# A weight ring of its own for the feed-forward part, with blocks that begin at an offset that changes from weight tile to weight tile

## The chip, the core and the metric

The kernel runs on one core of a Trainium2 chip. Five engines work side by side on that core and wait for each other through semaphores: TensorE (PE, matmuls; PEld is its weight load), VectorE (DVE), ScalarE (ACT), GpSimd (POOL) and SyncE (SP), which here issues every DMA. The metric is the device time of one execution in microseconds, the median of several runs. The kernel before takes 856.42 us.

## The reference

One decoder layer for 512 tokens of width 1024, all in float32. A token mixer (a pooling branch and a sparse attention branch, merged by gates) comes first; behind it stands the part that the change touches:

```python
def conv_ffn(h, w_up, conv_w, conv_b, w_down):
    S = h.shape[1]
    u = h @ w_up                                   # 1024 -> 2 x 2752
    up = jnp.pad(u, ((0, 0), (CONV_WIDTH - 1, 0), (0, 0)))
    c = conv_b + conv_w[0] * up[:, 0:S]
    for tap in range(1, CONV_WIDTH):
        c = c + conv_w[tap] * up[:, tap:tap + S]
    gate, val = jnp.split(c, 2, axis=-1)
    return (jax.nn.silu(gate) * val) @ w_down      # 2752 -> 1024
...
        x = x + token_mixer(h, ...)
        h = rms_norm(x, ffn_norm_w[l])
        x = x + conv_ffn(h, w_up[l], conv_w[l], conv_b[l], w_down[l])
```

## The kernel before

Activations lie transposed: a tile holds 128 channels by 512 tokens. Every large product is made of three matmuls on rounded halves: a value is split into `hi` (its rounding) and `lo` (the rest), and `mm3` (L103 to L109) adds hi·hi, hi·lo and lo·hi in one PSUM bank. The first operand of `pe.matmul` after the bank is the stationary one (128 by 128, loaded as weights); the second moves through it, up to 512 columns at a time.

**The weight ring.** `Ring` (L146) fetches one tile of weights (128 by 1024) by DMA into `st` (two buffers), and splits it in blocks of 512 columns: ACT writes `hi` (L95), DVE writes `lo` (L98). There are six `hi` and six `lo` buffers, so three tiles of weights are in flight. One ring serves the whole kernel; it lives in the pool `wr`, opened at the start.

**The stages at the end.** After the attention come, one after another on PE: `w_ab` (eight tiles, moving operand `oT`), `w_o` (eight tiles, moving operands `mh` and `ml`), the up projection `w_up` (43 tiles, moving operands `h2h` and `h2l`, called by `conv_tile`, L795), and the down projection `w_dn` (eight output tiles `c`, each of three fetches of seven 128-column blocks, moving operands `gh` and `gl`). The last output tile of `w_dn` is computed in two halves of 256 tokens. Output tile 7 of `w_o` is added to the residual (DVE L782), then split into `h2h7`, `h2l7`; the squares of all eight are summed on POOL (L212) for the norm, whose factors are applied only after the up projection (`rstdb`). So the up projection can begin before the norm is done, and with k = 0 to 6 before the last tile of `w_o` is done.

**Order.** The program is written in Python as above; the framework then orders each engine's instructions by a simulation of its own and puts in the waits. A buffer of a tag is free for its next writer when its last reader is done. A pool that is opened where a closed pool lay may write there only when the closed pool's readers are done.

**Addresses.** In the built program the buffers begin, in each partition, at these bytes: `hi` and `lo` blocks of the ring at 79,904 + 2,048 n; `oT` tiles at 32 bytes past a multiple of 512; `mh`, `ml` at 480 past a multiple of 512; `h2h`, `h2l` at multiples of 2,048; `gh`, `gl` at 32 past a multiple of 512. Earlier in the kernel `tok_gemm` (L304, matmuls `tg`) moves ring blocks of 256 columns past stationary activations `hh` and `hl`, which lie where `h2h` and `h2l` do later, and `cmp_hid` (matmuls `hp`, L461) moves ring blocks of 256 columns past the stationary `X`, whose slices begin at 480 past a multiple of 512. A 128-column weight block is 512 bytes of a partition, so the four blocks of one buffer begin at the same byte modulo 512 (79,904 is 32 past a multiple of 512).

Of the kernel before, what the change touches and what calls it, by code (L numbers as in the profile page):

```python
# [12 lines left out]
F32R = mybir.dt.float32r  # L13
# [6 lines left out]
P = 128  # L20
# [54 lines left out]
def layer(ctx: ExitStack, tc: tile.TileContext, par, masks, xT, w_kva, w_tm, w_fm, w_pl, w_pbr,  # L75
# [5 lines left out]
    def nm(s):  # L81
        cnt[0] += 1
        return f"{s}{cnt[0]}"

    def pool(stack, name, **kw):
        return stack.enter_context(tc.tile_pool(name=name, bufs=1, **kw))
# [4 lines left out]
    def split(hi, lo, src, scale=None, eng=None, cast=None):  # L91

        if scale is None:
            if cast is None:
                a.activation(hi, src, AF.Copy)  # L95
            else:
                cast.tensor_copy(hi, src)
            (eng or v).tensor_tensor(lo, src, r32(hi), ALU.subtract)  # L98
        else:
            a.activation(hi, src, AF.Copy, scale=scale)  # L100
            v.scalar_tensor_tensor(lo, src, scale, r32(hi), ALU.mult, ALU.subtract)

    def mm3(ps, pairs, first=True, last=True):  # L103

        n = len(pairs)
        for i, ((sh, sl), (mh_, ml_)) in enumerate(pairs):
            pe.matmul(ps, sh, mh_, start=first and i == 0, stop=False)  # L107
            pe.matmul(ps, sh, ml_, start=False, stop=False)  # L108
            pe.matmul(ps, sl, mh_, start=False, stop=last and i == n - 1)  # L109
# [2 lines left out]
    cp = pool(ctx, "cp")  # L112
    xp = pool(ctx, "xp")
    ypp = pool(ctx, "ypp")
    wr = pool(ctx, "wr")
    mix = ExitStack()
    qo = pool(mix, "qo")
    kvp = pool(mix, "kvp")
# [10 lines left out]
    def bank(p, tag, name, bufs):  # L129
        return p.tile([P, S], F32, tag=tag, name=nm(name), bufs=bufs)  # L130
# [13 lines left out]


    class Ring:  # L146
        def __init__(self, p, half, bufs):
            self.p, self.half, self.bufs = p, half, bufs

        def __call__(self, src, w, n, eng=None, cast=None):  # L150

            st = self.p.tile([P, 1024], F32, tag="st", name=nm("st"), bufs=self.bufs[0])
            nc.sync.dma_start(st[:, :n * w], src)
            out = []
            per = self.half // w
            for i in range(0, n, per):
                m = min(per, n - i)
                hi = self.p.tile([P, self.half], F32R, tag="hi", name=nm("hi"), bufs=self.bufs[1])
                lo = self.p.tile([P, self.half], F32R, tag="lo", name=nm("lo"), bufs=self.bufs[1])
                split(hi[:, :m * w], lo[:, :m * w], st[:, i * w:(i + m) * w], eng=eng, cast=cast)  # L160
                out += [(hi[:, j * w:(j + 1) * w], lo[:, j * w:(j + 1) * w]) for j in range(m)]
            return out

    ring = Ring(wr, 512, (2, 6))
# [590 lines left out]
    mh = [pq.tile([P, S], F32R, name=f"mh{c}") for c in range(8)]  # L755
    ml = [pq.tile([P, S], F32R, name=f"ml{c}") for c in range(8)]

    def fm2(src, ht, hl_):
        ps = bank(psm, "m", "fm", 6)
        mm3(ps, [(w, (ht[k], hl_[k])) for k, w in enumerate(ring(src, P, KC))])  # L760
        return ps

    for c in range(8):
        if c < NF1:
            z = sg1[c]
        else:
            z = sig2(fm2(w_fm[12 + c], hh, hl), pq.tile([P, S], F32, tag="zg", name=nm("zg"), bufs=2))
        ya = fm2(w_ab[c], oh, ol)
        v.scalar_tensor_tensor(z, z, 1.0, ya, ALU.add, ALU.mult)
        v.scalar_tensor_tensor(z, z, 0.5, ypool[c], ALU.mult, ALU.add)  # L770
        split(mh[c], ml[c], z)

    x1 = [ypp.tile([P, S], F32, tag=f"yp{c}", name=f"x1_{c}") for c in range(8)]
    h2h = [xp.tile([P, S], F32R, tag=f"hh{k}", name=f"h2h{k}") for k in range(KC)]
    h2l = [xp.tile([P, S], F32R, tag=f"hl{k}", name=f"h2l{k}") for k in range(KC)]
# [4 lines left out]
    for c in range(8):  # L780
        ps = fm2(w_o[c], mh, ml)
        v.tensor_tensor(x1[c], ps, x1[c], ALU.add)  # L782
        split(h2h[c], h2l[c], x1[c], fn[:, c:c + 1])
        sq_add(ssum, x1[c], c, pq, g, 4)
# [2 lines left out]
    mix.close()  # L787


    fp = pool(ctx, "fp")  # L790
    gh = [fp.tile([P, S], F32R, name=f"gh{j}") for j in range(NG - 1)]
    gl = [fp.tile([P, S], F32R, name=f"gl{j}") for j in range(NG - 1)]
    gs = fp.tile([P, S], F32R, name="gs")

    def conv_tile(t):  # L795
        ps = fm2(w_up[t], h2h, h2l)
        u = fp.tile([P, S], F32, tag="u", name=nm("u"), bufs=2)
        v.tensor_tensor(u, ps, rstdb, ALU.mult)
        c = fp.tile([P, S], F32, tag="c", name=nm("c"), bufs=3)
        a.activation(c, u, AF.Identity, bias=conv[:, t, 3:4], scale=conv[:, t, 2:3])  # L800
        v.scalar_tensor_tensor(c[:, 1:], u[:, :S - 1], conv[:, t, 1:2], c[:, 1:], ALU.mult, ALU.add)
        v.scalar_tensor_tensor(c[:, 2:], u[:, :S - 2], conv[:, t, 0:1], c[:, 2:], ALU.mult, ALU.add)
        return c

    for j in range(NG):
        if j == 0:
            c = conv_tile(0)
            rows = 64
            cv = fp.tile([P, S], F32, tag="c", name=nm("cv"), bufs=3)
            a.activation(cv[:64], c[64:128], AF.Copy)  # L810
            cg = c
        else:
            cg = conv_tile(2 * j - 1)
            cv = conv_tile(2 * j)
            rows = P
        a.activation(cg[:rows], cg[:rows], AF.Silu)
        v.tensor_tensor(cg[:rows], cg[:rows], cv[:rows], ALU.mult)
        if j == 0:
            split(gs[:64], gs[64:], cg[:64])
        else:  # L820
            split(gh[j - 1], gl[j - 1], cg)
# [7 lines left out]
    for c in range(8):  # L829
        sl = slice(c * P, (c + 1) * P)  # L830

        cols = [slice(0, S)] if c < 7 else [slice(h * S // 2, (h + 1) * S // 2) for h in range(2)]
        banks = [bank(psm, "m", "dn", 6) for _ in cols]
        ws = []
        for q_ in range(3):
            ws += ring(w_dn[c, :, q_ * 896:(q_ + 1) * 896], P, 7)
            if q_ < 2:
                for ps, cs in zip(banks, cols):
                    mm3(ps[:, cs], [(ws[k], (gh[k][:, cs], gl[k][:, cs])) for k in range(7 * q_, 7 * q_ + 7)],
                        first=q_ == 0, last=False)  # L840
        for ps, cs in zip(banks, cols):
            mm3(ps[:, cs], [(ws[k], (gh[k][:, cs], gl[k][:, cs])) for k in range(14, 21)], first=False, last=False)
            pe.matmul(ps[:, cs], wlh[:, sl], gs[:, cs], start=False, stop=False)
            pe.matmul(ps[:, cs], wll[:64, sl], gs[:64, cs], start=False, stop=True)
            o = fp.tile([P, S], F32, tag="o", name=nm("o"), bufs=2)
            v.tensor_tensor(o[:, cs], ps[:, cs], x1[c][:, cs], ALU.add)
            nc.sync.dma_start(outT[sl, cs], o[:, cs])
# [92 lines left out]
```

## Time and profile before

| | |
|---|---|
| median of 3 runs | 856.42 us (856.03 to 857.04) |
| profiled execution, its own time | 855.8 us |
| its span, first to last instruction | 853.9 us |
| PE busy | 837.8 us (98% of the span) |
| DVE, ACT, POOL busy | 566.4, 466.5, 235.5 us |
| mean granted TensorE clock | 0.996 of full speed |

The span is what the trace covers; the 1.9 us between span and time lie around it. A matmul's duration in the profile contains its way through the array, which overlaps with the next matmul's, so what a stream of matmuls costs is read from the distance of their starts. A granted clock of 1.0 is TensorE's upper level (2.4 GHz), 0.5 the lower one (1.2 GHz).

### The profile page before, as it was taken

Reading aid. Unit: us, or ns where it says so; the run is one execution under the profiler, and the core shown is the slowest. Engines: PE = TensorE matmul, PEld = TensorE weight load, DVE = VectorE, ACT = ScalarE, POOL = GpSimd, SP = SyncE. Lnnn points to the kernel's source line nnn. Section 1 sums busy time; section 2 is a strip of 40 time slices with the busy share of each in tenths; the row PEclk is TensorE's granted clock in tenths of the full one; section 3 lists DMA queues with packets and bytes.
Section 4 is the critical chain, followed back from the end, with each engine's and each line's share of the span. In section 5 each row is a group of like instructions: output and inputs, shape, how many; then the busy total and the mean of one; then the engine's idle time right before and its main releaser. Section 6 shows DMA issues by size and latency. Waiting matters only on the chain.

```text
span 853.9 us, 12252 instructions
## 1 busy us (share of the span) xinstructions
PE 837.8 (98%) x4355; PEld 700.9 (82%) x4355; DVE 566.4 (66%) x1203; ACT 466.5 (55%) x1002; POOL 235.5 (28%) x325
## 2 busy tenths in 40 slices
PE   7999899999999999999999999999999999999998
PEld 6889888978888888888888888888888888887887
DVE  7788967777787878785555539777777777423221
ACT  6846857768787877874334437545444444322220
POOL 5796714357565655640001200000000000000000
PEclk9999989999999999999999999999999999999999
DMA  6332132321001100101443223332233323333430
GB/s 218 102 119 91 51 102 96 103 96 50 26 26 47 30 25 26 47 28 50 148 148 99 98 74 100 99 98 83 91 100 98 99 85 104 111 108 99 111 98 25
DMA packets 22972, 72.82 MB, mean 85 GB/s; under 512 B 2816, under 2 KB 3328, under 8 KB 22912
## 3 DMA queue, kind: packets, MB, share of 16 engines
q1 hardware_dynamic: 22912, 72.05, 27.5%
q8 instruction: 34, 0.56, 0.3%
q14 instruction: 26, 0.21, 0.1%
HBM read 69.94 MB, written 2.10 MB: 84 GB/s over the span
## 4 chain that ended last, share of the span: by engine, by line
PE 84%; ACT 2%; DVE 1%; issue 1%; ACTq 0%; DVEq 0%
PE fm L107 16%; PE fm L108 16%; PE fm L109 16%; PE dn L107 5%; PE op L704 5%; PE dn L108 4%; PE dn L109 4%; PE tp L697 4%; PE ss L665 2%; PE ss L666 2%; PE op L709 1%; PE sc L608 1%; PE tg L312 1%; PE hp L461 1%; PE tg L310 1%; PE tg L311 1%
## 5 line engine op out<-in xcount | busy, mean ns | idle before, releaser
L95 ACT ACTIVATE hi<-st 128x512 fp32r<-128x512 f32 (+3 forms) x253 | 152.1, 607 | 202.2 <-PE fm L108 103.6
L98 DVE TENSOR_TENSOR lo<-st,hi 128x512 fp32r<-128x512 f32 (+1 forms) x210 | 141.8, 680 | 108.5 <-ACT hi L95 104.6
L107 PE MATMUL fm<-h2h,hi 128*128 128x512 f32 x344 | 136.1, 396 | 0.0
L108 PE MATMUL fm<-h2l,hi 128*128 128x512 f32 x344 | 136.0, 396 | 0.0
L109 PE MATMUL fm<-h2h,lo 128*128 128x512 f32 x344 | 135.9, 395 | 0.0
L677 POOL TENSOR_TENSOR pb<-pb,sm 128x128 f32<-128x128 f32 (+3 forms) x128 | 90.4, 738 | 49.3 <-DVE sm L674 40.4
L655 ACT ACTIVATE pb<-pb,nm 128x384 f32<-128x384 f32 (+3 forms) x128 | 71.1, 556 | 20.0 <-DVE nm L654 19.3
L107 PEld LDWEIGHTS fm<-h2h,hi 128*128 128x128 f32 x344 | 64.6, 188 | 15.7
L108 PEld LDWEIGHTS fm<-h2l,hi 128*128 128x128 f32 x344 | 64.6, 188 | 15.5
L109 PEld LDWEIGHTS fm<-h2h,lo 128*128 128x128 f32 x344 | 64.6, 188 | 15.5
L107 PE MATMUL fm<-hh,hi 128*128 128x512 f32 x160 | 71.6, 448 | 0.0
L107 PE MATMUL dn<-gh,hi 128*128 128x512 f32 (+1 forms) x189 | 69.9, 370 | 0.0
L108 PE MATMUL dn<-gl,hi 128*128 128x512 f32 (+1 forms) x189 | 69.1, 365 | 0.0
L109 PE MATMUL dn<-gh,lo 128*128 128x512 f32 (+1 forms) x189 | 69.1, 365 | 0.0
L98 DVE TENSOR_TENSOR ptl<-tp,pth 128x512 fp32r<-128x512 f32 (+1 forms) x96 | 57.2, 597 | 14.4 <-ACT pth L95 13.9
L654 DVE CUSTOM_DVE_ANT_0 pb<-ss,mk 128x384 f32<-128x384 f32 (+3 forms) x128 | 59.5, 482 | 8.5 <-PE ss L666 4.3
L108 PE MATMUL fm<-hl,hi 128*128 128x512 f32 x160 | 63.6, 397 | 0.0
L109 PE MATMUL fm<-hh,lo 128*128 128x512 f32 x160 | 63.0, 396 | 0.0
L95 ACT ACTIVATE pth<-tp 128x512 fp32r<-128x512 f32 (+1 forms) x96 | 49.8, 518 | 20.1 <-PE tp L697 19.7
L98 POOL TENSOR_TENSOR lo<-st,hi 128x512 fp32r<-128x512 f32 x36 | 48.5, 1350 | 34.4 <-ACT hi L95 34.4
L310 PE MATMUL tg<-hi,hh 128*128 128x256 f32 x192 | 54.1, 284 | 1.1 <-ACT h L288 1.1
L311 PE MATMUL tg<-hi,hl 128*128 128x256 f32 x192 | 53.6, 282 | 0.0
(256 smaller groups left out, 1838.4 us busy)
## 6 DMA issues: line engine op xcount, KB each, us to landing
st<-in_w_up SPq DMA_DIRECT2D x43, 512.0 KB, 3.5
st<-in_w_dn SPq DMA_DIRECT2D x24, 448.0 KB, 3.4
st<-in_w_fm SPq DMA_DIRECT2D x20, 512.0 KB, 3.5
st<-in_w_tm SPq DMA_DIRECT2D x12, 512.0 KB, 3.5
st<-in_w_ab SPq DMA_DIRECT2D x8, 512.0 KB, 3.4
st<-in_w_o SPq DMA_DIRECT2D x8, 512.0 KB, 3.5
x<-in_xT SPq DMA_DIRECT2D x15, 256.0 KB, 3.7
st<-in_cw SPq DMA_DIRECT2D x4, 512.0 KB, 3.7
```

The costliest lines, as they stand in the source:

```text
L95: a.activation(hi, src, AF.Copy)
L98: (eng or v).tensor_tensor(lo, src, r32(hi), ALU.subtract)
L107: pe.matmul(ps, sh, mh_, start=first and i == 0, stop=False)
L108: pe.matmul(ps, sh, ml_, start=False, stop=False)
L109: pe.matmul(ps, sl, mh_, start=False, stop=last and i == n - 1)
L310: pe.matmul(ps[:, :n], hh[k][:, tt], H, start=k == 0, stop=False)
L311: pe.matmul(ps[:, :n], hl[k][:, tt], H, start=False, stop=False)
L654: v.tensor_tensor_reduce(p_, ps, mcaus[:, S - n:], -1.0, 3e38, ALU.add, ALU.min, nm_[:, i:i + 1])
L655: a.activation(p_, p_, AF.Exp, bias=nm_[:, i:i + 1], scale=-1.0, accum_out=sm[:, i:i + 1])
L677: g.tensor_tensor(pb[:, PBASE[i]:PBASE[i] + n], pb[:, PBASE[i]:PBASE[i] + n], sm[:, i:i + 1].to_broadcast([P, n]), ALU.mult)
L697: last = pe.transpose(tp[:, n:n + P], pb[:, PBASE[i] + j * P:PBASE[i] + (j + 1) * P], ident)
L704: pe.matmul(op[:, j * P:], V2[b][j][:, G], pt_[:, TBASE[j]:TBASE[j] + w], start=b == 0 and j == 0 and part == 0, stop=False)
```

## The change

The old ring's pool is put on a stack of its own and closed after the mixer's pools; a new pool `wr2` is opened in its place and a new ring made in it, with the same numbers of buffers. A block of the new ring is 640 columns wide instead of 512, and `Ring.at` says at which of them the 512 used columns begin: `8 * (t // 3)` for tile `t` of `w_up` (0 to 112 columns, 0 to 448 bytes, a new value each time the ring has gone round), and `8 * c + 4` for output tile `c` of `w_dn` (4 to 60 columns, 16 to 240 bytes). What is computed is the same.

```diff
-    wr = pool(ctx, "wr")
+    wrs = ExitStack()
+    wr = pool(wrs, "wr")
...
     class Ring:
-        def __init__(self, p, half, bufs):
-            self.p, self.half, self.bufs = p, half, bufs
+        def __init__(self, p, half, bufs, pad=0):
+            self.p, self.half, self.bufs, self.pad, self.at = p, half, bufs, pad, 0
...
-                hi = self.p.tile([P, self.half], F32R, tag="hi", name=nm("hi"), bufs=self.bufs[1])
-                lo = self.p.tile([P, self.half], F32R, tag="lo", name=nm("lo"), bufs=self.bufs[1])
+                hi, lo = (self.p.tile([P, self.half + self.pad], F32R, tag=n_, name=nm(n_), bufs=self.bufs[1])[:, self.at:]
+                          for n_ in ("hi", "lo"))
...
-    def fm2(src, ht, hl_):
+    def fm2(src, ht, hl_, ring=ring):
...
     mix.close()
 
 
+    wrs.close()
+    wr = pool(ctx, "wr2")
+    ring = Ring(wr, 512, (2, 6), 128)
     fp = pool(ctx, "fp")
...
     def conv_tile(t):
-        ps = fm2(w_up[t], h2h, h2l)
+        ring.at = 8 * (t // 3)
+        ps = fm2(w_up[t], h2h, h2l, ring)
...
         banks = [bank(psm, "m", "dn", 6) for _ in cols]
+        ring.at = 8 * c + 4
         ws = []
```

In the built program of the change the ring's blocks begin at 79,904 + 2,560 n bytes plus the offset (2,560 is five times 512), `gh` and `gl` lie 6,144 bytes further on (twelve times 512), and `h2h`, `h2l` where they were.

**SP's queue, the last weights of `w_o` and the first of `w_up`, before** (a row is an instruction in program order; in brackets are the semaphores that it waits for, `DMAHW` those of earlier transfers):

```order
L153 DMA st_5787<-in_w_o 128x1024 [waits DMAHW5_49,DMAHW0_49,DVE_49]
L153 DMA st_5828<-in_w_o 128x1024 [waits DMAHW7_49,DVE_49]
L153 DMA st_5940<-in_w_up 128x1024 [waits DMAHW2_49,DMAHW0_49,DVE_49]
L153 DMA st_5987<-in_w_up 128x1024 [waits DMAHW1_49,DVE_49]
```

and with the change:

```order
L154 DMA st_5787<-in_w_o 128x1024 [waits DMAHW5_49,DMAHW0_49,DVE_49]
L154 DMA st_5828<-in_w_o 128x1024 [waits DMAHW7_49,DVE_49]
L154 DMA st_5944<-in_w_up 128x1024 [waits DMAHW1_49,DMAHW0_49,DMAHW2_49,DVE_49,PE_49]
L154 DMA st_5991<-in_w_up 128x1024
```

The order is the same; the first fetch for `w_up` now waits for PE as well, and the count that it waits for in the built program is the one that the last matmul of `w_o` raises (it reads the closed ring's last `lo` block). The second fetch follows without a wait of its own.

**ACT's queue at the same place, before** (`h2h` and `sq` are the rounding and the square of a finished tile of `w_o`; `hi` rounds weights that SP fetched to `st`):

```order
L95 ACTIVATE hi_5942<-st_5940 128x512 [waits DMAHW2_49,PE_49,Activation_49]
L95 ACTIVATE hi_5946<-st_5940 128x512 [waits PE_49,Activation_49]
L100 ACTIVATE h2h_5521<-x_5_5513,pk 128x512 [waits DVE_49]
L211 ACTIVATE sq_5783<-x_5_5513 128x512 [waits Pool_49]
L95 ACTIVATE hi_5989<-st_5987 128x512 [waits DMAHW3_49,PE_49,Activation_49]
L95 ACTIVATE hi_5993<-st_5987 128x512 [waits PE_49,Activation_49]
L100 ACTIVATE h2h_5522<-x_6_5514,pk 128x512 [waits DVE_49]
L211 ACTIVATE sq_5824<-x_6_5514 128x512 [waits Pool_49]
L95 ACTIVATE hi_6030<-st_6028 128x512 [waits DMAHW4_49,PE_49,Activation_49]
L95 ACTIVATE hi_6034<-st_6028 128x512 [waits PE_49,Activation_49]
L100 ACTIVATE h2h_5523<-x_7_5515,pk 128x512 [waits DVE_49]
```

and with the change:

```order
L100 ACTIVATE h2h_5521<-x_5_5513,pk 128x512 [waits DVE_49]
L212 ACTIVATE sq_5783<-x_5_5513 128x512 [waits Pool_49]
L100 ACTIVATE h2h_5522<-x_6_5514,pk 128x512 [waits DVE_49]
L212 ACTIVATE sq_5824<-x_6_5514 128x512 [waits Pool_49]
L100 ACTIVATE h2h_5523<-x_7_5515,pk 128x512 [waits DVE_49]
L212 ACTIVATE sq_5865<-x_7_5515 128x512 [waits Pool_49]
L95 ACTIVATE hi_5946<-st_5944 128x512 [waits DMAHW2_49,PE_49,Activation_49]
L95 ACTIVATE hi_5950<-st_5944 128x512
L95 ACTIVATE sh_5868<-ssum_5532 128x512 [waits Pool_49]
L95 ACTIVATE hi_5993<-st_5991 128x512 [waits DMAHW3_49]
```

The weights of the first three tiles of `w_up` were split between the last tiles of `w_o`; now the first of them stands behind all work on `w_o`.

## Rows read from the trace of the kernel before

**Rows 1.** The page: span, PE's busy time, granted clock in 40 slices.

```profile
span 853.9 us, 12252 instructions
...
PE 837.8 (98%) x4355; PEld 700.9 (82%) x4355; DVE 566.4 (66%) x1203; ACT 466.5 (55%) x1002; POOL 235.5 (28%) x325
...
PEclk9999989999999999999999999999999999999999
```

**Rows 2.** PE in stretches of `w_ab`, `w_o`, `w_up` (two), `w_dn`: busy (matmuls), clock, DMA.

```profile
400.00:440.00 40.00, 40.00 (x178) 1.00 0.44 143
445.00:485.00 40.00, 40.00 (x173) 1.00 0.33 107
520.00:560.00 40.00, 40.00 (x173) 1.00 0.35 105
...
680.00:720.00 40.00, 40.00 (x173) 1.00 0.34 102
...
745.00:758.00 13.00, 13.00 (x59) 1.00 0.45 127
```

**Rows 3.** Matmuls of `w_ab` and `w_o` by operand: duration, first and last start.

```profile
L107 PE MATMUL fm<-oT,hi x64: 389/389/395, 397.7 to 440.6; 128*128 128x512 f32 x64
...
L109 PE MATMUL fm<-oT,lo x64: 389/389/389, 398.2 to 441.0; 128*128 128x512 f32 x64
...
L107 PE MATMUL fm<-mh,hi x64: 394/394/394, 441.2 to 485.3; 128*128 128x512 f32 x64
L109 PE MATMUL fm<-mh,lo x64: 394/394/394, 441.7 to 485.8; 128*128 128x512 f32 x64
```

**Rows 4.** PE in order of time, 256-column matmuls of `w_dn` and `tg`.

```profile
839.82 0.28 PE L109 MATMUL dn<-gh,lo 128*128 128x256 f32 x1
...
840.90 0.28 PE L109 MATMUL dn<-gh,lo 128*128 128x256 f32 x1
...
41.06 0.28 PE L311 MATMUL tg<-hi,hl 128*128 128x256 f32 x1
...
43.62 0.28 PE L312 MATMUL tg<-lo,hh 128*128 128x256 f32 x1
```

**Rows 5.** All engines in order of time, last matmul of `w_o`, first of `w_up`.

```profile
485.81 0.39 PE L109 MATMUL fm<-mh,lo 128*128 128x512 f32 x1
...
486.05 0.40 PE L107 MATMUL fm<-h2h,hi 128*128 128x512 f32 x1
...
486.07 0.64 ACT L95 ACTIVATE hi<-st 128x512 fp32r<-128x512 f32 x1 [2.18 <-PE fm L108]
486.25 0.69 DVE L782 TENSOR_TENSOR x<-fm,x 128x512 f32<-128x512 f32 x1 [1.63 <-PE fm L109]
...
486.85 0.68 DVE L98 TENSOR_TENSOR lo<-st,hi 128x512 fp32r<-128x512 f32 x1
```

**Rows 6.** Fetches to `st` from 465 to 720 us: starts, and issue to landing.

```profile
L153 SPq DMA_DIRECT2D st<-in_w_up x43: 327/328/328, 465.2 to 702.3; - x43
...
DMA to landing us min/median/max: 3.3/3.5/4.5
```

**Rows 7.** ACT and POOL behind the last tile of `w_o`.

```profile
487.60 0.61 ACT L211 ACTIVATE sq<-x 128x512 f32<-128x512 f32 x1
...
488.36 1.29 POOL L212 TENSOR_TENSOR ssum<-ssum,sq 128x512 f32<-128x512 f32 x1 [4.31 <-ACT sq L211]
```

**Rows 8.** PE from 102.8 to 116.5 us, columns as in Rows 2.

```profile
102.80:106.20 3.40, 1.32 (x6) 1.00 0.00 0
106.20:109.60 3.40, 2.13 (x9) 0.51 0.60 175
109.60:113.10 3.50, 3.50 (x17) 0.50 0.33 130
113.10:116.50 3.40, 3.40 (x32) 1.00 0.61 167
```

**Rows 9.** PE around the idle time at 104 us, and `hp` at both clocks.

```profile
103.72 0.40 PE L109 MATMUL pl<-pli,plw 128*128 128x512 f32 x1
106.71 1.12 PE L361 MATMUL qt<-pk,qd 128*128 128x128 f32 x4 [2.59 <-DVE qp L365]
...
110.03 0.63 PE L461 MATMUL hp<-lo,X 128*128 128x256 f32 x2
...
112.59 0.63 PE L461 MATMUL hp<-lo,X 128*128 128x256 f32 x2
...
151.49 0.40 PE L461 MATMUL hp<-hi,X 128*128 128x256 f32 x2
...
153.14 0.40 PE L461 MATMUL hp<-lo,X 128*128 128x256 f32 x2
```

## The prediction

> **What bounds the kernel.** First the page: PE is busy for 837.8 of 853.9 us and the clock stands at full speed in all but one slice [rows 1]. So only PE's own stream counts, and the other engines only where PE waits for them. Then the stretches of PE [rows 2]: busy is 100% in `w_ab`, `w_o`, `w_up` and `w_dn` alike, and the reader is to look at the count of matmuls instead. 40 us hold 178 in `w_ab` and 173 in `w_o` and in both stretches of `w_up`; 13 us hold 59 in `w_dn`. (About 1.7 of each count were already under way at the start, a matmul lasting 0.39 us.) All are 512 columns wide, at the same clock. Starts lie apart by (441.0 - 397.7) / 191 = 226.7 ns in `w_ab` and (485.8 - 441.2) / 191 = 233.5 ns in `w_o` [rows 3]; the counts give 233.5 for `w_up` (40 / 171.3) and 226.9 for `w_dn` (13 / 57.3) [rows 2]. Two levels, some 226.7 and 233.3, are what the end of this kernel runs at.
>
> **What goes with the level.** Call lead the byte at which the moving operand begins, less that of the stationary one, modulo 512 (a stage's four blocks of a buffer lie 512 bytes apart, and all of them run alike, so only the rest can matter). By the addresses given, the lead is 0 in `w_ab` and `w_dn`, the fast stages, and 480 and 448 in `w_up` and `w_o`, the slow ones. Matmuls of 256 columns: at lead 0 in `w_dn`, (840.90 - 839.82) / 9 = 120 ns; in `tg`, where the ring's blocks move and the activations are stationary, the lead is 32, and (43.62 - 41.06) / 22 = 116.4 ns [rows 4]. In `hp` the same 256 columns take (153.14 - 151.49) / 14 = 117.9 ns [rows 9] at a lead of 64. So small positive leads seem 2 to 4 ns better than 0, small negative ones (480 is -32) 6.7 ns worse. That is a correlation over six stages; it is not shown that the lead is the cause.
>
> **The change, first part: the new ring's start.** The first fetch for `w_up` now waits for the last matmul of `w_o`. That starts at 485.81 and takes 0.39, so it ends at 486.20; DVE, which waits for the same event, starts at 486.25 [rows 5]. So SP issues at 486.25. A fetch lands 3.5 us later (3.3 to 4.5) [rows 6]: 489.75. ACT's `hi` takes 0.64 [rows 5], with 0.05 before and behind it: PE starts `w_up` at 490.5, where before it started at 486.05 [rows 5]. That is **4.4 us** of idle PE (4.2 to 5.4). Nothing covers it: everything behind it on PE is `w_up`, and it is waiting for the same weights. The other work of that moment is not later than the weights: DVE adds tile 7 from 486.25, `sq` follows 1.35 later and POOL's sum 0.76 after that, 1.29 long [rows 5, 7], so it ends at 489.7, and `sh` stands behind two `hi` on ACT; `nsum` comes 14 matmuls into `w_up`, which is at 493.8 at the earliest. If the clock stays up, PE waits a little more at its third matmul, which needs `lo`: 0.69 + 0.05 less two matmuls of 0.233, 0.3 us.
>
> Then the clock. The only long idle time in the trace is that from 104.12 (103.72 + 0.40) to 106.71 [rows 9]. The granted clock was at 2.4 GHz up to 106.2, and fell to 1.2 GHz (0.51, 0.50) from there to 113.1, though PE worked from 106.71 on, and fully from 109.6 on [rows 8]. At that clock `hp` took (112.59 - 110.03) / 12 = 213 ns [rows 9], against 117.9: a lost share of 0.45. The new idle time is 1.7 times as long as that one, so I expect the same: the fall 2.1 us into it, at 488.3, and the return 6.9 us later, at 495.2. PE works at the lower clock from 490.5 to 495.2 and loses 4.7 x 0.45 = **2.1 us** (0 if it does not fall, 6.9 x 0.45 = 3.1 if all of it falls on work). The start costs 6.5 us in all, between 4.5 (no fall, 4.2 + 0.3) and 8.5 (5.4 + 3.1).
>
> Later fetches are hidden again: a tile of 24 matmuls takes 5.6 us at 233 ns and a fetch 3.5, two fetches go out together, and splits are 1.3 us of ACT a tile.
>
> **Second part: the leads.** In `w_up` the lead becomes -(32 + 32 g), g = t // 3: tiles 0 to 23 go through -32 to -256, tiles 24 to 42 through 224 down to 32. In `w_dn` it becomes -(16 + 32 c), -16 to -240. The trace has only -32, -64, 0, 32 and 64. I take the negative half of the round as slow as its two known points (233.3) and the positive half as better than lead 0 by the 2 to 4 ns of the 256-column rows, say 2.7: 224.0. Then
> - tiles 0 to 23 of `w_up`: nothing changes.
> - tiles 24 to 42: 19 x 24 = 456 matmuls x (233.3 - 224.0) = -4.2 us.
> - `w_dn`, tiles 0 to 6: 7 x 63 = 441 matmuls x (233.3 - 226.7) = +2.9 us. Tile 7: 126 of 256 columns, none seen at a negative lead; between 0 and 126 x 6.7 = 0.8, I take 0.4.
>
> Together -0.9 us. Bounds from the two levels of 512 columns that the trace has: if all 37 tiles of `w_up` with new leads (888 matmuls) ran at 226.7 and `w_dn` stayed, -5.9 us; if none of `w_up` gained and all of `w_dn` lost, +3.7.
>
> Off PE nothing is added: the same instructions of the same sizes write the blocks, and DVE and ACT have slack.
>
> **Sum.** +6.5 - 0.9 = +5.6 us. The profiled execution took 855.8 us, its span 853.9; the change would make them 861.4 and 859.5. The median of the runs is 0.6 above the profiled time, so the forecast for it is 856.4 + 5.6 = **862.0 us**.
>
> **Rivals.**
> 1. *Addresses don't matter*, and the two levels come from something else that goes with the stage. For it: six stages only, and each differs in more than the lead. Against it: DVE, ACT and DMA load differ between `w_ab` and `w_dn`, which run alike. Only the start is left: +6.5, 862.9 us. The Trainium skill says as much, in "SBUF — State Buffer", section "Who interferes with whom": PE has one read port for the moving operand and an independent one for weight loads, and never waits on anyone. No row contradicts it directly; but two levels at one clock and one width ask for something that it doesn't name.
> 2. *The other side: a gain that pays for the start.* If leads other than the few negative ones near 0 were all as good as 32 and 64 look, 888 matmuls of `w_up` gain 9.3 ns (-8.3) and 441 of `w_dn` 2.7 (-1.2): 6.5 - 9.5 = -3.0, 853.4 us. It decides from a gain of 8.2 us on, which is 9.2 ns for each of the 888. For it: the 256-column rows. Against it: they are of other widths and other stages.
> 3. *Both known levels, the better one everywhere* (-5.9): 857.0 us.
> 4. *The sweep is bad*: `w_up` gains nowhere, `w_dn` loses everywhere: 856.4 + 6.5 + 3.7 = 866.6 us.
> 5. *The ring's start costs less*: if the fetch did not wait for the last matmul, or the clock held, 2 to 6 us less than each of these. The order speaks against the former, the idle time at 104 us against the latter.
>
> **How the numbers follow.** Forecast (start paid, part of `w_up` gains, `w_dn` loses) 0.42; rival 1 0.22, rival 2 0.11, rival 3 0.10, rival 4 0.10, rival 5 0.05. The range for 8 in 10 reaches from just under rival 3 to just below rival 4, 856.5 to 866.5; it takes in rival 1 and the bounds of the start around the forecast (860.0 to 864.0). The likeliest case's own range is 859 to 865. About 0.2%, 1.7 us, is what a measurement of this kernel can tell from no change: below 854.7 lie rival 2 and a bit of 5 (faster 0.12); between 854.7 and 858.1 rival 3 and a bit of 5 (same 0.13); the rest is slower, 0.75.
>
> **What the new profile would show.** Step 1: a stretch without matmuls from 486.2 to about 490.5, ended by ACT's `hi`, and SP's fetch issued at its start. Step 2: 0.5 in the granted clock from about 488 to 495. Step 3: starts of matmuls 233 ns apart in `w_up` up to tile 23, closer from tile 24 on; 233 in `w_dn` instead of 227. If the spacing is unchanged in every group of three tiles and in `w_dn`, rival 1 holds. The forecast fails most if the spacing as a function of the lead has another shape than two halves (a level below any seen, or one above), since each nanosecond on all 1,032 matmuls of `w_up` is 1 us.

## The result and the profile after

The change makes the kernel slower: 863.49 us (863.15 to 865.7) against 856.22 us for the kernel before, a ratio of 1.009 with a 95% interval of 1.0076 to 1.0104. That is 7.3 us, where 5.6 were forecast. The profiled execution has a span of 861.7 us, 7.8 more than before [rows 1].

The page of the kernel after, its span and PE's line:

```profile
span 861.7 us, 12246 instructions
...
PE 842.2 (98%) x4355; PEld 703.7 (82%) x4355; DVE 567.1 (66%) x1203; ACT 466.1 (54%) x1002; POOL 235.4 (27%) x325
```

The same 4,355 matmuls keep PE busy for 842.2 us in place of 837.8 [rows 1]: part of the loss is idle time, part is matmuls that take longer. (The page's sums don't divide it exactly: in the first 120 us PE is busy 1.2 us longer than before and idle 1.2 us less, and nothing is lost there. The stages below do.) The boundary between `w_o` and `w_up` shows the idle time. The kernel after, all engines in order of time; the end of a row says how long the engine was idle and what released it:

```profile
485.70 0.40 PE L109 MATMUL fm<-mh,lo 128*128 128x512 f32 x1
486.13 6.06 SPq L154 DMA_DIRECT2D st<-in_w_up  x3
...
489.88 1.15 ACT L95 ACTIVATE hi<-st 128x512 fp32r<-128x512 f32 x2 [1.78 <-DMA st<-in_w_up]
...
490.56 0.79 PE L107 MATMUL fm<-h2h,hi 128*128 128x512 f32 x1 [4.46 <-ACT hi L95]
```

SP's first fetch for `w_up` goes out at 486.13, when the last matmul of `w_o` has ended; ACT waits for its landing, and PE for ACT. The two matmuls start 4.86 us apart; before it was 486.05 - 485.81 = 0.24 [rows 5]. So 4.6 us.

PE of the kernel after in stretches; columns: stretch, its length, PE busy (matmuls), granted clock, DMA share, GB/s:

```profile
445.00:485.00 40.00, 40.00 (x173) 1.00 0.16 52
484.40:487.80 3.40, 1.70 (x8) 1.00 0.16 10
487.80:491.20 3.40, 0.64 (x2) 0.55 0.73 299
491.20:494.60 3.40, 3.40 (x10) 0.50 0.38 133
494.60:498.00 3.40, 3.40 (x16) 0.95 0.57 181
520.00:560.00 40.00, 40.00 (x173) 1.00 0.33 102
680.00:720.00 40.00, 40.00 (x174) 1.00 0.31 92
750.00:763.00 13.00, 13.00 (x58) 1.00 0.43 119
```

The clock is at the lower level, 1.2 GHz, from about 488.1 to about 494.9. Two matmuls of that time, five starts apart:

```profile
491.58 0.63 PE L109 MATMUL fm<-h2h,lo 128*128 128x512 f32 x1
...
493.71 0.63 PE L108 MATMUL fm<-h2l,hi 128*128 128x512 f32 x1
```

PE works from 490.56 on; at the lower level starts lie some 427 ns apart, (493.71 - 491.58) / 5, in place of 233. That is 4.4 us at a lost share of 0.45, 2.0 us.

The long stretches of `w_up` count as before, 173 and 174 [rows 2]. To see the leads one has to look at each group of three tiles. Single matmuls of the kernel after, PE in order of time: the first and the last of lead 288, of lead 256, of lead 64 (72 matmuls each), and of the first tile of `w_dn`, lead 496 (63 matmuls):

```profile
594.88 0.40 PE L107 MATMUL fm<-h2h,hi 128*128 128x512 f32 x1
...
611.45 0.39 PE L109 MATMUL fm<-h2h,lo 128*128 128x512 f32 x1
611.68 0.39 PE L107 MATMUL fm<-h2h,hi 128*128 128x512 f32 x1
...
627.77 0.40 PE L109 MATMUL fm<-h2h,lo 128*128 128x512 f32 x1
...
711.99 0.40 PE L107 MATMUL fm<-h2h,hi 128*128 128x512 f32 x1
...
728.25 0.39 PE L109 MATMUL fm<-h2h,lo 128*128 128x512 f32 x1
...
734.09 0.40 PE L107 MATMUL dn<-gh,hi 128*128 128x512 f32 x1
...
748.56 0.40 PE L109 MATMUL dn<-gh,lo 128*128 128x512 f32 x1
```

16.57 / 71 = 233.4 ns at 288, 16.09 / 71 = 226.6 at 256, 16.26 / 71 = 229.0 at 64, and 14.47 / 62 = 233.4 in `w_dn`, which ran at 226.9 before. Worked out in the same way for every group (mean distance of starts, gaps that a wait made left out; good to about 0.2 ns):

| lead modulo 256 | 0 | 32 | 64 | 96 | 128 | 160 | 192 | 224 |
|---|---|---|---|---|---|---|---|---|
| `w_up`, lead below 256, ns | (none) | 233.3 | 229.1 | 233.4 | 232.4 | 234.2 | 233.4 | 233.2 |
| `w_up`, lead from 256 on, ns | 226.8 | 233.3 | 229.1 | 233.4 | 232.4 | 234.2 | 233.4 | 232.8 |

| `w_dn`, lead modulo 256 | 240 | 208 | 176 | 144 | 112 | 80 | 48 |
|---|---|---|---|---|---|---|---|
| ns | 233.4 | 233.2 | 231.9 | 233.2 | 233.3 | 230.0 | 233.3 |

The two rows of `w_up` are the same: the spacing repeats after 256 bytes, not 512, and of eight leads two are good. By stage, from its first matmul to the first of the next: idle time +4.6, `w_up` 242.55 to 243.53 (+1.0: +2.0 of clock, -1.0 of leads), `w_dn` 121.88 to 124.19 (+2.3, to the start of its last matmul). `w_o` ended 0.1 earlier. The sum, 4.6 + 1.0 + 2.3 - 0.1 = 7.8, is the whole difference of the spans.

### The profile page after: what moved, and what is told of

Its sections match the earlier page's. It is cut to its first block, busy times and chain, and to the rows that moved or that the text cites. A ratio compares the mean times of both kernels' runs of the same rounds, so it can differ in the third digit from the quotient of the medians.

```text
span 861.7 us, 12246 instructions
## 1 busy us (share of the span) xinstructions
PE 842.2 (98%) x4355; PEld 703.7 (82%) x4355; DVE 567.1 (66%) x1203; ACT 466.1 (54%) x1002; POOL 235.4 (27%) x325
## 4 chain that ended last, share of the span: by engine, by line
PE 83%; ACT 2%; DVE 1%; issue 1%; DMA 0%; ACTq 0%; DVEq 0%
PE fm L107 16%; PE fm L108 16%; PE fm L109 16%; PE dn L107 5%; PE dn L108 5%; PE dn L109 5%; PE op L705 5%; PE tp L698 4%; PE ss L666 2%; PE ss L667 2%; PE op L710 1%; PE sc L609 1%; PE tg L313 1%; PE tg L311 1%; PE hp L462 1%; PE tg L312 1%
```

## The experiments

Forecast and first rival lie close together (862.0 and 862.9), and the time alone doesn't tell them apart. The first four kernels separate the start of the ring from the leads. Where rows give a stage's length below, they are the matmuls by operand: shortest, median and longest duration in ns, first and last start. For the kernel before the first row of `w_up` runs from 486.0 to 727.9, 241.9 us.

**e1: the ring without the sweep.** Against the kernel after:

```diff
-        ring.at = 8 * (t // 3)
         ps = fm2(w_up[t], h2h, h2l, ring)
...
-        ring.at = 8 * c + 4
```

> The new ring with its wider blocks is kept, but its offset stays 0, so the leads are those of before (480 in w_up, 0 in w_dn). Theory A (start of the ring and lead are two separate terms): only the start is paid, 4.6 us of idle PE and 2.0 us of lower clock, 856.2 + 6.6 = 862.8 us; w_up matmuls start 233.3 ns apart again in all tiles, and w_dn falls back from 124.2 to 121.9 us; so the kernel of the change is about 0.7 us slower than this one. Rival B (the spacing in w_dn rose because the ring lies elsewhere or has wider blocks, not because of the offset): w_dn stays at 124.2 us and w_up at the spacing that the change shows, 863.5 us.

Measured: 863.55 us (862.43 to 864.01), ratio 1.0081 (1.0067 to 1.0095). The kernel e1, matmuls of `w_up` and `w_dn` by operand:

```profile
L107 PE MATMUL fm<-h2h,hi x344: 392/396/792, 491.3 to 735.8; 128*128 128x512 f32 x172
...
L107 PE MATMUL dn<-gh,hi x189: 279/389/496, 736.5 to 857.8; 128*128 128x512 f32 x147, 128*128 128x256 f32 x42
```

`w_dn` takes 121.86 us again, so its loss of 2.3 us comes from the offset, not from the ring's place or its wider blocks: rival B falls. `w_up` spans 244.5, 2.6 more than before at the same spacing of 233.3 ns: that is the clock, 0.6 more than in the kernel after, since here the lower level came and went later. The kernel e1, PE in stretches, columns as above:

```profile
487.80:491.20 3.40, 0.00 (x0) 0.83 0.83 307
491.20:494.60 3.40, 3.34 (x8) 0.50 0.24 58
494.60:498.00 3.40, 3.40 (x12) 0.67 0.74 257
```

The expected 0.7 us between this kernel and that of the change can't be seen in the medians (863.55 and 863.49). In the two stages the traces differ by about as much (367.06 and 367.72 us for `w_up` and `w_dn` together), but not for the expected reason: the offsets cost the kernel after 1.3 us there, and e1 loses 0.6 more to the lower clock.

**e5: the ring with a constant, good lead.** Against the kernel after:

```diff
-        ring.at = 8 * (t // 3)
+        ring.at = 56
...
-        ring.at = 8 * c + 4
+        ring.at = 0
```

> The new ring with a constant offset of 56 columns (224 bytes) in w_up, which makes its lead 256, and offset 0 in w_dn (lead 0). Theory A (spacing is a function of the lead with a period of 256 bytes): 1,032 matmuls at 226.7 in place of 233.3 ns gain 6.8 us, which pays for the start: 862.8 - 6.8 = 856.0 us, and w_up from first to first matmul of w_dn takes about 237.7 us where e1 has 244.5. The prediction's own reading of the lead (modulo 512, its positive half good by the 256-column rows) gives nothing for 256, the middle of the round: about 862.8. Rival B (place, not lead): 862.8 to 863.5 us.

Measured: 856.86 us (855.31 to 857.26), ratio 1.0002 (0.9993 to 1.001), no difference from before. The kernel e5, the same row:

```profile
L107 PE MATMUL fm<-h2h,hi x344: 387/389/794, 491.2 to 729.1; 128*128 128x512 f32 x172
```

237.9 us against e1's 244.5: 6.6 us from one constant. Theory A holds, and the prediction's round of 512 bytes falls, since 256 was its middle.

**e3: no second ring, only a shift.** Against the kernel before:

```diff
+    ypp.tile([P, 56], F32, name="pad")
     wr = pool(ctx, "wr")
```

> The kernel of before, without a second ring: one unused tile of 56 columns (224 bytes) ahead of the ring moves the ring and all that is laid out behind it, so the lead modulo 256 becomes 0 in w_up (1,032 matmuls) and in the fm matmuls of the mixer on hh (480), 224 in w_o (was 192), 0 in tg (was 32), and stays 0 in w_ab and w_dn. Theory A: w_up gains 6.8 us, the 480 of the mixer up to 3.2, tg (576 of 256 columns) may lose 3.6 ns each, 2.1 in all: 856.2 - 6.8 - 3.2 + 2.1 = 848.3 us, between 846 and 850, with no idle PE between w_o and w_up. Rival B (place or the second ring decides): 856.2, no change.

Measured: 849.73 us (848.96 to 850.2), ratio 0.9921 (0.9908 to 0.9933). **e4** adds the second tile:

```diff
     norm_scales(ssum, rt2, pq, (bank_g, bank_g, bank_g), 4)
+    pq.tile([P, 56], F32, name="pad2")
     post.close()
```

> The kernel e3 and one more unused tile of 56 columns in the pool of mh and ml, which makes the lead 0 in w_o too. Theory A: 192 matmuls of w_o at 226.7 in place of 233.3 ns, 1.3 us less than e3, about 847.0 us; w_o from first to last matmul 43.3 in place of 44.6 us. Rival (w_o's level is its own, from what DVE and ACT do there): no change from e3.

Measured: 848.12 us (847.98 to 848.16), ratio 0.9903 (0.989 to 0.9917). The kernel e3, matmuls of `w_up` and `w_o` by operand:

```profile
L107 PE MATMUL fm<-h2h,hi x344: 387/389/478, 487.1 to 722.3; 128*128 128x512 f32 x172
...
L109 PE MATMUL fm<-mh,lo x64: 395/396/396, 442.7 to 486.8; 128*128 128x512 f32 x64
```

The kernel e4, the same:

```profile
L107 PE MATMUL fm<-h2h,hi x344: 389/389/478, 485.1 to 720.3; 128*128 128x512 f32 x172
...
L109 PE MATMUL fm<-mh,lo x64: 389/389/389, 442.1 to 484.9; 128*128 128x512 f32 x64
```

`w_up` falls to 235.2 us in both (6.7 less than before). `w_o` keeps 44.1 (first to last start of its `lo` matmuls) in e3, as before [rows 3], and falls to 42.8 in e4, when `mh` and `ml` move and the ring stays. So it is the one address less the other that counts: for `w_up` e3 moved the stationary side, for `w_o` e4 moved the moving one, and `w_ab`, where e3 moved both alike, stays at 226.7 ns. The mixer gave nothing to e3, where up to 3.2 less 2.1 was expected: its `tg` matmuls went from 116.9 to 119.7 ns, as the two 256-column rows said [rows 4], and its `fm` matmuls from 232.9 to 230.4 only, not to 226.7; why isn't shown.

**e6: matmuls that fill the idle time.** Added to e1, with a result that nobody reads:

```diff
+    fill = bank(psm, "m", "fill", 6)
+    for i in range(17):
+        pe.matmul(fill, ones, h2h[6], start=i == 0, stop=i == 16)
     wrs.close()
```

> The kernel e1 and 17 extra matmuls ahead of the first one of w_up, on operands that are ready and into a bank that nobody reads, so that PE works through most of the time in which the new ring waits for its first weights. Theory A (the clock fell because PE stood idle, and the fall is a cost of its own): the granted clock stays at 1.0 from 488 to 495, w_up takes 242.6 us where e1 has 245.2, and the time is 863.5 - 2.6 = 860.9 us, with the first matmul of w_up no earlier. Rival C (the clock falls there whatever PE does, or the loss is in the first weights coming late): no change from e1, 863.5 us.

Measured: 861.51 us (860.07 to 861.73), ratio 1.0057 (1.0043 to 1.0071). The kernel e6, the boundary on PE in order of time:

```profile
486.31 0.40 PE L109 MATMUL fm<-mh,lo 128*128 128x512 f32 x1
486.54 4.14 PE L793 MATMUL fill<-h2h,ones 128*128 128x512 f32 x17
491.30 0.50 PE L107 MATMUL fm<-h2h,hi 128*128 128x512 f32 x1 [0.62 <-ACT hi L95]
```

And its PE in stretches:

```profile
487.80:491.20 3.40, 2.88 (x13) 1.00 0.76 296
491.20:494.60 3.40, 3.30 (x13) 1.00 0.27 92
494.60:498.00 3.40, 3.40 (x17) 1.00 0.70 223
```

The weights still arrive 5 us after the last matmul of `w_o`, but the clock holds, and `w_up` takes 242.94 us in place of e1's 245.20. The lower clock is a cost of its own, about 2 us, and PE's idleness is what brought it on.

**e7 and e11: the leads in steps of 8 bytes**, twice the same kernel; **e10**: in reverse order. Against the kernel after (`84 - 2 * t` in e10):

```diff
-        ring.at = 8 * (t // 3)
+        ring.at = 2 * t
...
-        ring.at = 8 * c + 4
+        ring.at = 0
```

> The new ring with an offset of 2 t columns in tile t of w_up: the lead goes down from 480 in steps of 8 bytes through 144 (tile 42), once round 256 and more; w_dn has lead 0. Theory A (period of 256 bytes): tiles 28 (lead 256) at 226.7 ns, tiles 20 (320) at 229.1, the multiples of 32 that the change showed repeated (tile 0 480, 4 448, 8 416, 12 384, 16 352, 24 288, 32 224, 36 192, 40 160 at 232 to 234), and tiles 8 bytes to either side of 256 tell how near the lead has to come: if only the residue 0 itself is good, tiles 27 and 29 are at about 233; if it is a matter of 32 bytes, tiles 25 to 31 come down in steps. With one to seven of 43 tiles gaining, 862.5 to 863.5 us. If the spacing depends on the number of the tile or the place in the ring and not on the lead, no tile stands out.

> The fine sweep e7 with its order turned round: offset 84 - 2 t columns in tile t, so the same 43 leads from 144 up to 480. Theory A (the lead alone sets the level): each lead has the spacing that it had in e7, whatever tile and place it now falls on; 392 at 227.0, 256 at 226.7, 272 at 228.3, 320 at 229.0, the rest at 230 to 234. Theory D (several steady patterns are possible at a lead, and the way into a tile, by the tile before it or by a disturbance of the stream, picks one): 256 keeps 226.7, but some leads change level, first of all 472 and 480, which in e7 came right behind the low clock and the norm's matmul and ran at 227 though 480 ran at 233.3 in e1 and 216 (the same as 472 modulo 256) at 233.0 in e7.

> The fine sweep e7 once more, unchanged. If what picks the level in a tile is fixed by the program (theory A, or theory D with a way in that is always the same), all 43 tiles repeat to about 0.5 ns. If chance picks it (theory D with small differences of time at the way in, such as the moment at which the clock returns), the tiles 0 and 1 (leads 480 and 472), and perhaps 11 (392), fall on another level than in e7 (227.0, 227.6 and 227.0 there), while 256 stays at 226.7.

Measured: 862.85, 862.87 (e11) and 861.84 us (e10), one time each. The mean distance of starts in a tile, from its tenth matmul on, in ns, at the leads that bear on the question (gaps at the lower clock or beside a matmul of the norm left out):

```
lead   480   472   392   384   320   296   272   264   256   248   232   216   160
e7   232.6 227.4 227.0 232.5 229.0 231.6 228.2 233.2 226.7 231.1 229.9 233.1 234.2
e11  232.0 227.4 227.0 232.5 229.0 231.6 228.2 233.2 226.7 231.1 229.9 233.1 234.2
e10  233.2 227.3 227.1 233.2 229.2 226.9 228.7 233.1 227.2 231.0 231.3 227.3 234.1
```

The kernel e7, PE in order of time: the tenth and the last matmul of the tiles with lead 264, 256 and 248, 14 starts apart each:

```profile
648.31 0.40 PE L107 MATMUL fm<-h2h,hi 128*128 128x512 f32 x1
...
651.58 0.39 PE L109 MATMUL fm<-h2h,lo 128*128 128x512 f32 x1
...
653.87 0.39 PE L107 MATMUL fm<-h2h,hi 128*128 128x512 f32 x1
...
657.04 0.39 PE L109 MATMUL fm<-h2h,lo 128*128 128x512 f32 x1
...
659.35 0.39 PE L107 MATMUL fm<-h2h,hi 128*128 128x512 f32 x1
...
662.58 0.40 PE L109 MATMUL fm<-h2h,lo 128*128 128x512 f32 x1
```

Eight bytes off 256 cost 6.5 ns on one side and 4.4 on the other, so a near miss is no near gain. Nor is 256 the only good lead: 392 (136 modulo 256) has 227.0 in all three kernels. e11 repeats e7 in every tile but the first to 0.1 ns: nothing here points to chance. With the order reversed, 40 of 43 leads keep their level within about 1.4 ns, whatever tile they fall on. Two don't: 296 (231.6 and 226.9) and 216 (233.1 and 227.3; 472, the same modulo 256, has 227 in all three).

The third is 480. The two expectations above take 227.0 for it in e7, but that isn't its level through the tile. The kernel e7, PE in order of time: the 15th and the 22nd matmul of that tile, a matmul of the norm, the 23rd, and the 21st of the next tile (lead 472):

```profile
497.62 0.40 PE L109 MATMUL fm<-h2h,lo 128*128 128x512 f32 x1
...
499.25 0.40 PE L107 MATMUL fm<-h2h,hi 128*128 128x512 f32 x1
499.49 0.39 PE L195 MATMUL nsum<-sl,ones 128*128 128x512 f32 x1
499.72 0.39 PE L108 MATMUL fm<-h2l,hi 128*128 128x512 f32 x1
...
504.70 0.39 PE L109 MATMUL fm<-h2h,lo 128*128 128x512 f32 x1
```

Once the clock is back, lead 480 runs at (499.25 - 497.62) / 7 = 233 ns or a little more, as in e1 and e10. Behind the single matmul of the norm (L195) the last two distances of this tile and the twenty that follow at lead 472 are (504.70 - 499.72) / 22 = 226 to 227 ns, until the norm's next matmuls at 504.94. So the lead sets the level nearly everywhere, and at a few leads the matmuls before it do too. Theory A falls short for these leads; the second pattern that theory D allows shows at none of the others.

**e8: one of three matmuls out of step.** Against e5:

```diff
-                hi, lo = (self.p.tile([P, self.half + self.pad], F32R, tag=n_, name=nm(n_), bufs=self.bufs[1])[:, self.at:]
+                hi, lo = (self.p.tile([P, self.half + self.pad], F32R, tag=n_, name=nm(n_), bufs=self.bufs[1])[:, (self.at if n_ == "hi" else 0):]
```

> The kernel e5, but with the lo blocks of w_up at offset 0: of each three matmuls the two on hi have lead 256 and the one on lo has lead 480 (at the same lead for every three of 24). Theory A1 (each matmul's own lead sets its spacing, or its neighbour's does): a third of the loss is back, 226.7 + 6.6 / 3 = 228.9 ns in the mean, w_up 240.7 us, 859.1 us in all; the start after the lo matmul is late if the own lead counts, the start of the lo matmul if it is the lead against the weights loaded next. Theory A2 (one matmul out of step throws the stream off for several): the mean goes most of the way to 233.3, w_up up to 245.2, up to 863.5 us.

Measured: 862.15 us, one time. The kernel e8, matmuls of `w_up` by operand:

```profile
L107 PE MATMUL fm<-h2h,hi x344: 389/395/795, 490.1 to 734.1; 128*128 128x512 f32 x172
```

244.0 us, against 237.9 in e5 and 244.5 in e1. Two thirds of the matmuls have the good lead, and nothing of the gain is left: the distances go round 232.5, 239, 228.5 ns, in the mean 233.3. Theory A2 holds for this mix: with one matmul in three at lead 480, the stream doesn't keep the good spacing.

**e9: the leads of e4 with `tg` as before.** All of `hh`, `hl`, `h2h`, `h2l` in one buffer; against the kernel before:

```diff
-    hh = [xp.tile([P, S], F32R, tag=f"hh{k}", name=f"hh{k}") for k in range(KC)]
-    hl = [xp.tile([P, S], F32R, tag=f"hl{k}", name=f"hl{k}") for k in range(KC)]
+    HX = xp.tile([P, 2 * KC * S + 64], F32R, name="HX")
+    hx = lambda i, at: HX[:, at + i * S:at + (i + 1) * S]
+    hh = [hx(k, 0) for k in range(KC)]
+    hl = [hx(KC + k, 0) for k in range(KC)]
...
-    h2h = [xp.tile([P, S], F32R, tag=f"hh{k}", name=f"h2h{k}") for k in range(KC)]
-    h2l = [xp.tile([P, S], F32R, tag=f"hl{k}", name=f"h2l{k}") for k in range(KC)]
+    h2h = [hx(k, 8) for k in range(KC)]
+    h2l = [hx(KC + k, 8) for k in range(KC)]
...
+    pq.tile([P, 48], F32, name="pad2")
```

> The leads of e4 in w_ab, w_o, w_up and w_dn (all 0 modulo 256), but the ring left at its place against hh, so that tg keeps lead 32: h2h and h2l are laid 8 columns (32 bytes) on from hh and hl in one buffer, and mh and ml moved by 48 columns. Theory A: against e4 the 576 matmuls of tg start 116.9 in place of 119.7 ns apart, 1.6 us less; the 480 fm matmuls of the mixer go back from lead 0 to 224, where e4's gain was 1.3 to 4 ns each, 0.6 to 1.9 us more; together 0 to 1 us less than e4, about 847.5 us (846.5 to 849). If the mixer is set by other engines than PE, exactly as e4, 848.1.

Measured: 848.06 us (847.84 to 848.76), ratio 0.9905 (0.9891 to 0.9918), the same as e4. For `w_up` it is now the moving side that was shifted, and it takes 235.6 us from its first matmul to its last, as in e3 and e4 (235.7 and 235.6). `tg` is back at 116.9 ns and the `fm` matmuls of the mixer at 232.9. Whether the two cancel or the mixer isn't set by PE's spacing stays open.

## Why the prediction was right, and where it wasn't

- **The start of the ring** was forecast at 4.4 us of idle time and 2.1 us of lower clock. Measured: 4.6 and 2.0 in the kernel after, and e6 shows that the second is caused by the first. That the 2.0 comes so near to 2.1 is partly luck: the fall came 2.0 us into the idle time in the kernel after and 3.1 us into it in e1, so that PE worked at the lower clock for 4.4 and 5.6 us, at a loss of 2.0 and 2.6. The chain SP, landing, `hi`, first matmul ran as laid out [rows 5, 6]; the fetch was 0.1 to 0.2 us slower than its median. The 0.3 us for `lo` was not seen as a wait.
- **The lead as the cause** was a correlation over six stages. e5, e3 and e4 show it: with the start of the ring or without it, by the stationary side or the moving one, spacing followed the lead. Rival 1 (addresses don't matter) falls, though its time, 862.9 us, was the nearest to the one measured. The Trainium skill's "SBUF — State Buffer", section "Who interferes with whom", gives the moving operand and the weight load a read port each, independent of one another, and says that PE never waits on anyone; it doesn't speak of addresses, which rival 1 took it to rule out. Read so, it would have e3 and e4 at 856.2 us, and they took 849.7 and 848.1.
- **The size of the leads** is the step that failed: -4.2 us for tiles 24 to 42 and +3.3 for `w_dn`, -0.9 in all. Measured: about -1.0 in `w_up` and +2.3 in `w_dn`, +1.3. The step read the round of 512 bytes as two halves, the positive one better than lead 0, from rows of 256 columns at 32 and 64. There is no good half. At 512 columns only 0 and, by some 4 ns, 64 are good among the multiples of 32, so of 19 tiles three gained 4.2 ns a matmul (lead 64), and of the first 24, which were to stay, lead 256 gained 6.6 and lead 320 4.2 over three tiles each: 72 x (4.2 + 6.6 + 4.2) = 1.1 us. The 256-column rows didn't mislead about themselves (`tg` lost 2.8 ns a matmul when e3 took it from 32 to 256, which is 0 modulo 256); they don't carry over to 512 columns.
- **`w_dn`** lost 2.3 of the 3.3 us forecast: leads 80 and 176 (tiles 2 and 5 of it) are a little better than the rest, and the last tile's 256-column matmuls, now at lead 272, went from 119.8 to 117.3 ns, a gain of 0.3 us where a loss of 0.4 had been taken.
- **Rivals 2 and 3**, a gain of 8.3 and 5.9 us in `w_up`, had the right size for an offset that is right in every tile: e5 gained 6.6 us with one, and came out level with before, as rival 3 said with 857.0. The change's sweep passes through that offset for 3 of 43 tiles (g = 7).
- The sum of the leads, +1.3, lies between the forecast's -0.9 and rival 4's +3.7, as the time, 863.5 us, lies between their 862.0 and 866.6. The net effect of the leads came out with the other sign than forecast; that the time still lies near it is owed to the start, which was sized rightly and outweighs them, and to luck in that the leads' effects are small in sum. Rival 5 (a cheaper start) falls with the rows of the boundary.

## What to carry over

When one shape of matmul at one clock shows two spacings in two stages, compare the byte at which the moving operand begins with that of the stationary one, and set the difference exactly, for all matmuls of the stream, to a value that a run has shown to be good (here 0 modulo 256). Here one unused tile of 224 bytes ahead of a buffer gained 6.5 us and a second one 1.6, where an offset that changes from tile to tile gained 1.0 and lost 2.3. Before a pool is closed and reopened between two stages, price the first load behind it: 4.6 us of waiting and 2 us of the lower clock here. A rule read off rows of one width (256 columns) is no estimate for another (512) until a row of that width shows it.

## What the hardware showed

- 512-column matmuls with new weights each time start 226.7 ns apart at the best leads (0 and 136 modulo 256) and near 233.3 at most others, at the higher clock. At the lower clock they start 427 ns apart, which is one column per period of 1.2 GHz and nothing more, with lead 480 (e1) and with lead 256 (e5) alike: between these two the lead costs only at the higher clock. There one column per period of 2.4 GHz would be 213.3 ns, so 13.3 or 20 are added.
- At a few leads two levels are possible (231.6 or 226.9 ns at 296, 233.1 or 227.3 at 216), and what ran before picks one: the tile before, or a single matmul of the norm, as at the step from 234 to 227 ns in e7. It was the same one in both runs of that program (e7, e11). What lies behind this wasn't settled; no run here separates a conflict of two reads from some other coupling of the weight load with the moving operand.
